# A two-layer hybrid block: the feed-forward's down product by Strassen's scheme over squares kept in DRAM, and the states of the linear attention formed before its outputs

## The chip, the cores and the metric

The kernel runs on one core of a Trainium2 chip. The metric is the time of one execution on the device in microseconds (us), as the median of several runs.

## The reference

The input is 1024 tokens of width 1024, in float32. Two layers of a first block and one layer of a second block follow each other. A layer of the first block mixes tokens (gated linear attention and latent softmax attention) and then has a feed-forward part with squared ReLU. The change lies in the feed-forward and in the linear attention of this block.

```python
def first_block(x, c, positions, ...):
    cos, sin = rope_tables(positions)
    for l in range(DEPTH):                                   # DEPTH = 2
        shift_a, scale_a, gate_a, shift_f, scale_f, gate_f = ...
        h = rms_norm(x) * (1.0 + scale_a) + shift_a
        x = x + gate_a * hybrid_mixer(h, cos, sin, ...)
        h = rms_norm(x) * (1.0 + scale_f) + shift_f
        x = x + gate_f * (jnp.square(jax.nn.relu(h @ w_mlp_up[l])) @ w_mlp_down[l])

# linear attention, chunk by chunk (heads of 64 keys and 128 values):
#   o = (q exp(b)) state + attn v;   state = exp(b_last) state + k_dec^T v
```

`w_mlp_up` is 1024 x 4096 and `w_mlp_down` 4096 x 1024 in each layer. The second block (dilated attention and long convolutions) is not touched.

## The kernel before

Activations lie transposed: 8 tiles of 128 features, each in two halves of 512 tokens (`hf`). Every large product is made from three matmuls: an operand is split into a high part (`split_hi`, ACT) and the rest (`split_lo`, a subtraction, POOL unless told otherwise), and high x high, high x low and low x high are summed in PSUM. One matmul covers 128 x 128 weights and 512 tokens.

The program is traced in the order of the source and a planner then orders each engine's instructions by readiness in its own model of time, with ties to the earlier one. On the chip each engine runs its list in that fixed order and waits on semaphores. DMAs are issued from SP's queue and from ACT's queue.

The feed-forward is `mlp`, called at the end of `layer1`. It goes through the 4096 hidden features in 16 chunks of 256. For a chunk, `up_weights` loads and splits two 1024 x 128 blocks of weights, `up_part` makes four products of 24 matmuls, takes ReLU (ACT), multiplies by the PSUM value (DVE) and splits the square at once (ACT, POOL). `down_weights` loads and splits two 128 x 1024 blocks, and `down_part` makes 16 products of 6 matmuls, each of which DVE scales by a gate and adds to the residual `x[f, hf]`. The down part of a chunk runs behind the up part of the next, so that up and down alternate; the last chunk is written out by hand, with `state[0](0)`, the norm of token half 0 for the next layer (`enter`), in between.

Linear attention is `gla`: 8 steps over (256 tokens, head pair). A step runs `gla_chunks` for this step with `gla_decays` of the next step beside it, and one piece of the mixer's output projection (`project_out`) is drawn in at every yield. In `gla_chunks` two chunks of 128 tokens follow each other (`cc`): score matmuls into `A`, evictions into `scores`, output products into `o_ps`, outer products into `u_ps`, from which DVE forms the new state. The two `u_ps` products of a chunk share one PSUM bank, and each is read by DVE before the next is written.

The rope tables (`rope_tables`) stay in SBUF through both layers.

Of the kernel before, what the change touches and what calls it, by code (L numbers as in the profile page):

```python
# [147 lines left out]
class Kernel:  # L148
# [285 lines left out]
    def block1(self):  # L434
        nc, i = self.nc, self.i
        self.mods = {}
        cond = self.cond_cols(i["c"], True, "1")
        cond2 = self.cond_cols(i["c_2"], False, "2")
        self.ada = {"0": (cond, i["w_ada"][0], i["b_ada"][0]), "1": (cond, i["w_ada"][1], i["b_ada"][1]),
                    "2": (cond2, i["w_ada_2"][0], i["b_ada_2"][0])}  # L440
        self.eps5 = self.C.tile([128, 1], F32, name="eps5")
        nc.gpsimd.memset(self.eps5, 1e-5)
        rp, rclose = self.open("rope", "right")
        xp, xclose = self.open("x0", "right")
        with self.pool("mod_0", "right") as p:
            x = self.load_x(xp)
            self.rope_tables(rp)
            self.main_tables()

            self.rstds = {hf: self.norm_rstd(p, x, hf, keep=2) for hf in range(2)}  # L450
            self.drain(self.modulation(p, "0", (0, 1), 10, True))
            state = self.enter("a0", x, self.mods["0", 1], self.mods["0", 0])
            self.first_weights(0)
            for hf in range(2):
                state[0](hf)
        for l in range(2):
            nxt = (lambda x, w: self.enter("a1", x, self.mods["1", 1], self.mods["1", 0], wclose=w)) if l == 0 else \
# [3 lines left out]
            state, xclose = self.layer1(l, state, xclose, nxt)  # L461
        xclose()
        rclose()
        return state

    def layer1(self, l, state, xclose, enter_next):
        nc, i = self.nc, self.i
        _, H, xs, close = state
        xclose()
        mixd = self.DR.tile([2, 8, 2, 128, 512], F32, name=f"mix{l}")  # L470

        ap, aclose = self.open("mla_in", "right")
        A = self.project_latent(l, H, ap)
# [14 lines left out]
        with self.pool("mod") as p:  # L488
            mods = (("0", (2, 3, 4, 5)), ("1", (0, 1))) if l == 0 else (("1", (2, 3, 4, 5)), ("2", (0, 1, 2)))
            fill = (None for name, secs in mods for _ in self.modulation(p, name, secs))  # L490
            steps = 8 * sum(len(secs) for _, secs in mods)
# [11 lines left out]
            for n in range(34):  # L503
                h, i = divmod(n, 8)
# [8 lines left out]
                if n > 1:  # L513
                    h, i = divmod(n - 2, 8)
# [6 lines left out]
        tclose()  # L521
        paclose()
        aclose()

        xp, xclose = self.open("x", "right")
        xa = {(f, hf): xp.tile([128, 512], F32, name=f"xa{f}_{hf}") for hf in range(2) for f in range(NF)}
# [25 lines left out]

        mp, mpclose = self.open("mlp", "right")
        hp, hclose = self.open("h2_0")
        hq, hqclose = self.open("h2_1", "right")
        H = {}
        self.h_tiles(H, hp, "f", 0)
        self.h_tiles(H, hq, "f", 1)
# [8 lines left out]
        def close():  # L567
            hclose()
            return enter_next(xa, wclose)

        return self.mlp(l, H, xa, gate_f, mp, close, lambda: (hqclose(), mpclose())), xclose

    def project_out(self, l, mp, mixd, part, xa, gate, tag, bufs, halves=(0, 1)):

# [22 lines left out]
        for _ in steps:  # L597
            pass

    def mlp(self, l, H, x, gate, p, close, pclose):  # L600

        nc, i = self.nc, self.i
        up, down = i["w_mlp_up"][l], i["w_mlp_down"][l]
        pt, ptclose = self.open("mlp_even", "right")

        def up_part(c, w, mt, hf):
            ps = self.PS.tile([128, 512], F32, name="up", tag="mm", bufs=2)
            self.gemm(ps, w[mt], slice(0, 128), lambda k, h: H[k, h], 8, hf)
            sq = p.tile([128, 512], F32, name="relu2", tag="relu2", bufs=2)
            nc.scalar.activation(sq, ps, AF.Relu)  # L610
            nc.vector.tensor_mul(sq, ps, sq)  # L611
            hi, lo = ((p if c % 2 else pt).tile([128, 512], F32R, name="act", tag=f"act{b}", bufs=4) for b in range(2))
            self.split_hi(hi, sq)
            self.split_lo(lo, sq, hi)
            return hi, lo

        def down_weights(c):
            dw = []
            for mt in range(2):
                n0 = c * 256 + mt * 128  # L620
                raw = pt.tile([128, 1024], F32, name="dn_raw", tag="dnr", bufs=2)
                nc.sync.dma_start(raw, down[n0 : n0 + 128, :])
                hi = p.tile([128, 1024], F32R, name="dn_hi", tag="dnh", bufs=3)
                lo = p.tile([128, 1024], F32R, name="dn_lo", tag="dnl", bufs=3)
                self.split_hi(hi, raw)
                self.split_lo(lo, raw, hi)
                dw.append((hi, lo))
            return dw

        def down_part(dw, act, hf):  # L630
            for f in range(NF):
                ps = self.PS.tile([128, 512], F32, name="dn", tag="dn", bufs=4)
                n = 0
                for mt in range(2):
                    (wh, wl), (ah, al) = dw[mt], act[mt, hf]
                    for a, b in ((wh, ah), (wh, al), (wl, ah)):
                        self.mm(ps, a[:, f * 128 : (f + 1) * 128], b, n == 0, n == 5)
                        n += 1
                nc.vector.scalar_tensor_tensor(x[f, hf], ps, gate[:, f : f + 1], x[f, hf], op0=ALU.mult, op1=ALU.add)  # L639
# [5 lines left out]
        behind = None  # L645
        for c in range(15):
            w, act = up_weights(c), {}

            for mt, hf in ((0, 0), (1, 0), (0, 1), (1, 1)) if c == 0 else ((0, 0), (0, 1), (1, 0), (1, 1)):
                act[mt, hf] = up_part(c, w, mt, hf)  # L650
            if behind:
                for hf in range(2):
                    down_part(*behind, hf)
            behind = down_weights(c), act
        w, act = up_weights(15), {}
        for mt in range(2):
            act[mt, 0] = up_part(15, w, mt, 0)
        for hf in range(2):
            down_part(*behind, hf)
        dw = down_weights(15)  # L660
        ptclose()
        state = close()
        down_part(dw, act, 0)
        state[0](0)
        for mt in range(2):
            act[mt, 1] = up_part(15, w, mt, 1)
        down_part(dw, act, 1)
        pclose()
        self.psum(f"ps_in{l}")
        state[0](1)  # L670
        return state
# [159 lines left out]
    def gla_setup(self, l, p, A):  # L831
# [15 lines left out]
        for b in range(2):  # L847
            nc.gpsimd.memset(heads[64 * b : 64 * b + 64, b : b + 1], 1.0)

        G["state"] = [[p.tile([128, 2, 128], F32, name=f"state{hp}_{n}") for n in range(2)] for hp in range(2)]  # L850
# [80 lines left out]
    def gla_chunks(self, p, G, oT, g, hp):  # L931
# [19 lines left out]
        group = []  # L951
        for cc in range(2):
            c = 2 * g + cc
            ct = slice(cc * 128, cc * 128 + 128)
            S_prev, sn = G["state"][hp][c % 2], G["state"][hp][1 - c % 2]

            z = G.pop(("z", g, hp, cc))
            ps = self.PS.tile([128, 1024], F32, name="A", tag="big", bufs=2)
# [15 lines left out]
            if cc:  # L974
                yield
            for b in range(2):
                h = 2 * hp + b
                if c:
                    group.append(self.mm(o_ps[:, b, cc, :], S_prev[:, b], e[:, cc, 7, :], True, False))
                group.append(self.mm(o_ps[:, b, cc, :], v[:, cc, h * 128 : h * 128 + 128], a[:, b], c == 0, True))  # L980
            if c < 7:
                u_ps = self.PS.tile([128, 128], F32, name="u_ps", tag="sm", bufs=2, padded_shape=[128, 512])
                for b in range(2):
                    r = slice(64 * b, 64 * b + 64)
                    h = 2 * hp + b
                    self.mm(u_ps[r], kd[:, cc * 128 + b * 64 : cc * 128 + b * 64 + 64], v[:, cc, h * 128 : h * 128 + 128],
                            True, True, tile_position=(0, 64 * b))
                    if c == 0:
                        nc.vector.tensor_copy(sn[r, b], u_ps[r])
                    else:  # L990
                        nc.vector.scalar_tensor_tensor(sn[r, b], S_prev[r, b], el[r, cc : cc + 1], u_ps[r], op0=ALU.mult, op1=ALU.add)
        self.in_order(group)
        for b in range(2):
            h = 2 * hp + b
# [1108 lines left out]
```

## Time and profile before

| | |
|---|---|
| median of 3 runs | 4408.63 us (4402.69 to 4411.74) |
| profiled execution, its own time | 4400.58 us |
| its span, first to last instruction | 4398.7 us |
| mean granted clock of the tensor engine | 0.966 |
| instructions | 52184 |

The profile is one execution. Its page has busy times by engine; the views behind it group instructions by line and shape, list them in order of time, sum up what waited for what, and give busy time by window. PE is the tensor engine's matmuls, PEld its weight loads (beside the matmuls), DVE VectorE, ACT ScalarE, POOL GpSimd, SP the engine whose queue issues most DMAs. Matmuls overlap in the pipeline, so the duration of one is longer than the distance from one start to the next.

### The profile page before, as it was taken

The numbers are of one execution on the slowest core, as the hardware profiler recorded it, in microseconds if no ns is written. First come the engines' busy times: TensorE is split into PE (matmuls) and PEld (weight loads), VectorE is DVE, ScalarE is ACT, GpSimd is POOL, SyncE is SP. The second block draws the span as 40 slices with busy tenths as digits, with TensorE's granted clock in tenths as the row PEclk, the third lists the DMA queues.
The fourth block names the chain that finished last, engine by engine and source line by source line (L and its number), as shares of the span: only waits on it lengthen the run. The fifth ranks groups of instructions, "written<-read, shape, count | busy, mean of one in ns | idle before, by whom it ended". The sixth has DMA issues, their size and how long they took to land. (4 is left out here: it accounts for less than half of the span.)

```text
span 4398.7 us, 52184 instructions
## 1 busy us (share of the span) xinstructions
PE 4077.9 (93%) x19748; PEld 3195.0 (73%) x19748; DVE 2020.7 (46%) x3789; ACT 1447.4 (33%) x2722; POOL 1419.1 (32%) x1309
## 2 busy tenths in 40 slices
PE   6999888999999999888999999899999999899788
PEld 3776666888887685566788888567777777778666
DVE  5427675333334515577433333652221444567446
ACT  5435354121212525444312121322223445211222
POOL 3322455333333422155433333212221111244242
PEclk8999899999999999999999999999999999999899
DMA  6245543111111126643211111144445332444353
GB/s 188 68 135 159 161 131 106 47 49 48 48 48 42 55 84 196 178 136 116 78 47 49 48 48 44 61 123 116 117 103 138 101 94 78 139 144 143 130 180 110
DMA packets 566222, 449.84 MB, mean 102 GB/s; under 512 B 197384, under 2 KB 468702, under 8 KB 565970
## 3 DMA queue, kind: packets, MB, share of 16 engines
q1 hardware_dynamic: 375514, 352.68, 26.3%
q10 hardware_dynamic: 189880, 92.63, 7.3%
q8 instruction: 156, 2.56, 0.2%
q0 software_dynamic: 576, 1.18, 0.1%
q14 instruction: 96, 0.79, 0.1%
HBM read 342.87 MB, written 100.92 MB: 101 GB/s over the span
## 5 line engine op out<-in xcount | busy, mean ns | idle before, releaser
L200 POOL TENSOR_TENSOR w_lo<-w_raw,w_hi 128x1024 fp32r<-128x1024 f32 (+4 forms) x237 | 449.1, 1896 | 1132.7 <-ACT w_hi L194 1111.1
L191 PE MATMUL dn<-act,dn_hi 128*128 128x512 f32 x2048 | 637.5, 392 | 14.5 <-DVE xa L639 6.0
L639 DVE SCALAR_TENSOR_TENSOR xa<-dn,mod,xa 128x512 f32<-128x512 f32 x512 | 383.7, 750 | 273.0 <-PE dn L191 271.2
L191 PE MATMUL in<-b2h,w_hi 128*128 128x512 f32 x1152 | 474.5, 412 | 5.6 <-ACT qkv_t L1650 5.6
L194 ACT ACTIVATE w_hi<-w_raw 128x1024 fp32r<-128x1024 f32 (+4 forms) x276 | 237.1, 860 | 710.6 <-PE in L191 271.5
L191 PE MATMUL in<-b2l,w_hi 128*128 128x512 f32 x1152 | 459.7, 399 | 0.0
L191 PEld LDWEIGHTS dn<-act,dn_hi 128*128 128x128 f32 x2048 | 386.8, 189 | 100.1 <-DVE xa L639 7.6
L191 PE MATMUL in<-b2h,w_lo 128*128 128x512 f32 x1152 | 458.4, 398 | 0.0
L191 PE MATMUL up<-fh,w_hi 128*128 128x512 f32 x1024 | 406.8, 397 | 0.4 <-DVE relu L611 0.4
L191 PE MATMUL up<-fl,w_hi 128*128 128x512 f32 x1024 | 404.0, 395 | 1.6 <-POOL fl L200 1.3
L191 PE MATMUL dn<-act,dn_lo 128*128 128x512 f32 x1024 | 402.0, 393 | 2.8 <-POOL dn_lo L200 2.8
L191 PE MATMUL up<-fh,w_lo 128*128 128x512 f32 x1024 | 404.2, 395 | 0.0
L611 DVE TENSOR_TENSOR relu<-up,relu 128x512 f32<-128x512 f32 x128 | 88.5, 691 | 610.1 <-ACT relu L610 610.1
L200 POOL TENSOR_TENSOR dn_lo<-dn_raw,dn_hi 128x1024 fp32r<-128x1024 f32 x64 | 152.1, 2398 | 525.1 <-ACT dn_hi L194 525.0
L191 PEld LDWEIGHTS in<-b2h,w_hi 128*128 128x128 f32 x1152 | 221.5, 192 | 64.6 <-issue 12.2
L191 PEld LDWEIGHTS in<-b2h,w_lo 128*128 128x128 f32 x1152 | 220.8, 192 | 53.4 <-issue 6.4
L191 PEld LDWEIGHTS in<-b2l,w_hi 128*128 128x128 f32 x1152 | 221.4, 192 | 47.4 <-issue 4.4
L194 ACT ACTIVATE dn_hi<-dn_raw 128x1024 fp32r<-128x1024 f32 x64 | 64.8, 1053 | 554.3 <-PE dn L191 546.8
L191 PEld LDWEIGHTS up<-fl,w_hi 128*128 128x128 f32 x1024 | 192.8, 188 | 49.2 <-POOL fl L200 3.0
L191 PEld LDWEIGHTS up<-fh,w_hi 128*128 128x128 f32 x1024 | 192.9, 188 | 46.3 <-issue 1.7
L191 PEld LDWEIGHTS dn<-act,dn_lo 128*128 128x128 f32 x1024 | 193.9, 189 | 44.5 <-POOL dn_lo L200 3.6
L191 PEld LDWEIGHTS up<-fh,w_lo 128*128 128x128 f32 x1024 | 192.9, 188 | 45.5 <-issue 1.0
(488 smaller groups left out, 7871.1 us busy)
## 6 DMA issues: line engine op xcount, KB each, us to landing
wada<-in_w_ada SPq DMA_DIRECT2D x120, 512.0 KB
w_raw<-in_w_in SPq DMA_DIRECT2D x102, 512.0 KB
w_raw<-in_w_mlp_up SPq DMA_DIRECT2D x64, 512.0 KB
dn_raw<-in_w_mlp_down SPq DMA_DIRECT2D x64, 512.0 KB
qkv<-qkv_t ACTq DMA_DIRECT2D x72, 256.0 KB
w_raw<-in_w_out SPq DMA_DIRECT2D x64, 256.0 KB
mix<-mix SPq DMA_DIRECT2D x64, 256.0 KB
spectra<-spec ACTq DMA_DIRECT2D x32, 384.0 KB
```

The costliest lines, as they stand in the source:

```text
L191: return self.nc.tensor.matmul(out, lhsT, rhs, start=start, stop=stop, **kw)
L194: self.nc.scalar.activation(hi, x, AF.Copy, **kw)
L200: return eng.tensor_sub(lo, x, hi.bitcast(F32))
L611: nc.vector.tensor_mul(sq, ps, sq)
L639: nc.vector.scalar_tensor_tensor(x[f, hf], ps, gate[:, f : f + 1], x[f, hf], op0=ALU.mult, op1=ALU.add)
```

## The change

The feed-forward falls into two parts. First all 16 chunks of the up product run, and their squares are written to a DRAM tensor `actd` from ACT's queue, unsplit. Then the down product runs over blocks of 512 hidden features: `raws` loads four weight blocks `A[m, k]` (output half, contraction half) and four blocks of squares `B[k, t]` (contraction half, token half). For seven blocks `products` forms Strassen's seven pairs (Winograd's form, with eight sums and differences on DVE) and `exact` splits every operand, in a ring of three buffers, two pairs ahead of the matmuls. Each pair gives 4 tiles of 6 matmuls, which DVE adds to 28 accumulators `acc` (ACT copies them for the first block). The eighth block is multiplied plainly, and the accumulators are combined in between (`self.plus`, which shares sums between DVE and POOL by a running count of cost, and `gated`).

In the linear attention the outer products and state updates of both chunks of a step move ahead of the second chunk's scores, and all output products come after the yield. A third state buffer holds the state in between.

For room in SBUF the rope tables go to DRAM at the start, are closed before the linear attention of layer 0, and are loaded again for layer 1.

```diff
+            self.rope_spill = self.DR.tile([2, 128, S], F32, name="rope_spill")
+            for n, t in enumerate((self.rc, self.rs)):
+                nc.scalar.dma_start(self.rope_spill[n], t)
...
+        if l:
+            rp, rclose = self.open("rope", "right")
...
+            for n, t in enumerate((self.rc, self.rs)):
+                nc.sync.dma_start(t, self.rope_spill[n])
...
+        actd = self.DR.tile([32, 2, 128, 512], F32, name=f"act{l}")
...
+        def up_part(kt, w, hf):
+            ps = self.PS.tile([128, 512], F32, name="up", tag="dn", bufs=4)
             self.gemm(ps, w, slice(0, 128), lambda k, h: H[k, h], 8, hf)
+            sq = sp.tile([128, 512], F32, name="relu2", tag="relu2", bufs=4)
             nc.scalar.activation(sq, ps, AF.Relu)
             nc.vector.tensor_mul(sq, ps, sq)
-            self.split_hi(hi, sq)
-            self.split_lo(lo, sq, hi)
+            nc.scalar.dma_start(actd[kt, hf], sq)
...
+        def raws(c):
+            A, B = {}, {}
+            yield A, B
+            for m, k, t in ((0, 0, 0), (0, 1, 0), (1, 1, 1), (1, 0, 1)):
+                kt = 4 * c + 2 * k
+                pool, tag, bufs = (dp, "dnr", 3) if m == 0 else (self.W, "wr", 2) if k else (dp, "dnr1", 2)
+                A[m, k] = pool.tile([128, 2, 512], F32, name="dn_raw", tag=tag, bufs=bufs)
+                nc.sync.dma_start(A[m, k], down[kt * 128 : kt * 128 + 256, m * 512 : m * 512 + 512].rearrange("(j p) n -> p j n", p=128))
+                B[k, t] = dp.tile([128, 2, 512], F32, name="sq_raw", tag="sqr", bufs=6)
+                nc.sync.dma_start(B[k, t], actd[kt : kt + 2, t].rearrange("j p n -> p j n"))
+                yield
...
+        def products(A, B):
+            V = nc.vector
+            yield 0, exact("a", A[0, 0], lo_vector=True), exact("b", B[0, 0], lo_vector=True)
+            yield 1, exact("a", A[0, 1]), exact("b", B[1, 0])
+            a22, b22 = exact("a", A[1, 1]), exact("b22", B[1, 1], True)
+            V.tensor_sub(B[0, 0], B[0, 1], B[0, 0])
+            V.tensor_sub(B[0, 1], B[1, 1], B[0, 1])
+            V.tensor_sub(B[1, 1], B[1, 1], B[0, 0])
+            V.tensor_sub(B[1, 0], B[1, 0], B[1, 1])
+            yield 3, a22, exact("b", B[1, 0])
+            V.tensor_add(A[1, 1], A[1, 0], A[1, 1])
+            V.tensor_sub(A[1, 0], A[0, 0], A[1, 0])
+            V.tensor_sub(A[0, 0], A[1, 1], A[0, 0])
+            V.tensor_sub(A[0, 1], A[0, 1], A[0, 0])
+            yield 2, exact("a", A[0, 1]), b22
+            yield 4, exact("a", A[1, 1]), exact("b", B[0, 0])
+            yield 5, exact("a", A[0, 0]), exact("b", B[1, 1])
+            yield 6, exact("a", A[1, 0]), exact("b", B[0, 1])
...
+        def work(c, p, w, a):
+            for f in range(4):
+                ps = multiply(f, [(w, a)])
+                if c:
+                    nc.vector.tensor_add(acc[p, f], ps, acc[p, f])
+                else:
+                    nc.scalar.activation(acc[p, f], ps, AF.Copy)
...
+        for f in range(4):
+            self.plus(acc[1, f], acc[0, f], acc[1, f])
+            gated(f, 0, acc[1, f])
+            self.plus(acc[5, f], acc[0, f], acc[5, f])
+            self.plus(acc[6, f], acc[5, f], acc[6, f])
+            self.plus(acc[3, f], acc[6, f], acc[3, f])
+            gated(4 + f, 0, acc[3, f])
+        for f in range(4):
+            plain(f, 0)
+        wa[1, 0], wa[1, 1], sb[0, 1] = exact("a", A[1, 0]), exact("a22", A[1, 1], True), exact("b", B[0, 1])
+        for f in range(4, 8):
+            plain(f, 0)
+        for f in range(4):
+            self.plus(acc[5, f], acc[4, f], acc[5, f])
+            self.plus(acc[2, f], acc[5, f], acc[2, f])
+            gated(f, 1, acc[2, f])
+            self.plus(acc[6, f], acc[4, f], acc[6, f])
+            gated(4 + f, 1, acc[6, f])
...
+        state = enter_next()
         state[0](0)
+        sb[1, 1] = exact("b", B[1, 1])
+        for f in range(8):
+            plain(f, 1)
```

In `gla_chunks`:

```diff
-            S_prev, sn = G["state"][hp][c % 2], G["state"][hp][1 - c % 2]
...
+            scores.append(a)
+            if cc == 0:
+                for c in (2 * g, 2 * g + 1):
+                    S_prev, sn = states[c % 3], states[(c + 1) % 3]
+                    if c == 7:
+                        break
+                    u_ps = self.PS.tile([128, 128], F32, name="u_ps", tag="sm", bufs=2, padded_shape=[128, 512])
+                    for b in range(2):
...
+        yield
+        for cc in range(2):
+            c = 2 * g + cc
             for b in range(2):
                 h = 2 * hp + b
                 if c:
+                    group.append(self.mm(o_ps[:, b, cc, :], states[c % 3][:, b], e[:, cc, 7, :], True, False))
+                group.append(self.mm(o_ps[:, b, cc, :], v[:, cc, h * 128 : h * 128 + 128], scores[cc][:, b], c == 0, True))
```

## Rows read from the trace of the kernel before

**Rows 1.** The page: busy us, share of the span, instructions, by engine.
```profile
PE 4077.9 (93%) x19748; PEld 3195.0 (73%) x19748; DVE 2020.7 (46%) x3789; ACT 1447.4 (33%) x2722; POOL 1419.1 (32%) x1309
```

**Rows 2.** By window, layer 1: stretch, us; PE, PEld, DVE, ACT, POOL; clock, DMA.
```profile
2200.00:2400.00 200.00, 200.00 (x876) 164.05 (x875) 67.72 (x92) 38.57 (x52) 64.66 (x35) 1.00 0.16 48
```

**Rows 3.** Timeline of ACT (start, us, what): a weight split in two following chunks.
```profile
1310.84 1.06 ACT L194 ACTIVATE dn_hi<-dn_raw 128x1024 fp32r<-128x1024 f32 x1 [18.18 <-PE dn L191]
...
1354.79 1.06 ACT L194 ACTIVATE dn_hi<-dn_raw 128x1024 fp32r<-128x1024 f32 x1 [18.18 <-PE dn L191]
```

**Rows 4.** Groups by line and shape: count, busy us, mean ns, idle before.
```profile
L639 DVE SCALAR_TENSOR_TENSOR xa<-dn,mod,xa 128x512 f32<-128x512 f32 x512 | 383.7, 750 | 273.0 <-PE dn L191 271.2
L611 DVE TENSOR_TENSOR relu<-up,relu 128x512 f32<-128x512 f32 x128 | 88.5, 691 | 610.1 <-ACT relu L610 610.1
L200 DVE TENSOR_TENSOR w_lo<-w_raw,w_hi 128x1024 fp32r<-128x1024 f32 x28 | 34.3, 1225 | 227.2 <-ACT w_hi L194 227.2
L1540 DVE TENSOR_TENSOR nacc<-nacc,nsq 128x512 f32<-128x512 f32 x27 | 22.8, 845 | 1.2
L200 POOL TENSOR_TENSOR act<-relu,act 128x512 fp32r<-128x512 f32 x128 | 168.1, 1314 | 171.0 <-ACT act L194 171.0
L200 POOL TENSOR_TENSOR dn_lo<-dn_raw,dn_hi 128x1024 fp32r<-128x1024 f32 x64 | 152.1, 2398 | 525.1 <-ACT dn_hi L194 525.0
L194 ACT ACTIVATE dn_hi<-dn_raw 128x1024 fp32r<-128x1024 f32 x64 | 64.8, 1053 | 554.3 <-PE dn L191 546.8 <-DMA dn_raw<-in_w_mlp_down 7.5
```

**Rows 5.** Timelines of POOL and DVE where both run, layer 0 of the feed-forward.
```profile
1413.80 1.70 POOL L200 TENSOR_TENSOR a1l<-nt,a1h 128x512 fp32r<-128x512 f32 x1 [3.23 <-ACT a1h L194]
1415.47 1.71 POOL L200 TENSOR_TENSOR act<-relu,act 128x512 fp32r<-128x512 f32 x1
1417.14 2.82 POOL L200 TENSOR_TENSOR w_lo<-w_raw,w_hi 128x1024 fp32r<-128x1024 f32 x1
...
1412.37 0.74 DVE L307 SCALAR_TENSOR_TENSOR a1l<-nt,mod,a1h 128x512 fp32r<-128x512 f32 x1
...
1414.29 6.22 DVE L299 SCALAR_TENSOR_TENSOR nt<-xa,s_a,rstd 128x512 f32<-128x512 f32 x3
...
1334.86 2.41 POOL L200 TENSOR_TENSOR w_lo<-w_raw,w_hi 128x1024 fp32r<-128x1024 f32 x1 [3.14 <-ACT w_hi L194]
...
1335.85 1.55 DVE L639 SCALAR_TENSOR_TENSOR xa<-dn,mod,xa 128x512 f32<-128x512 f32 x2
```

**Rows 6.** PE after two waits near the end of layer 0, and windows behind.
```profile
1391.10 0.50 PE L191 MATMUL dn<-act,dn_lo 128*128 128x512 f32 x1 [1.38 <-POOL dn_lo L200]
...
1417.23 0.80 PE L191 MATMUL dn<-act,dn_hi 128*128 128x512 f32 x1 [2.30 <-POOL act L200]
...
1392.00:1400.00 8.00, 8.00 (x37) 6.62 (x36) 6.94 (x11) 3.78 (x6) 0.00 (x0) 1.00 0.46 170
1418.00:1421.00 3.00, 3.00 (x9) 2.33 (x8) 3.00 (x2) 1.46 (x3) 3.00 (x2) 0.50 0.00 0
1430.00:1436.00 6.00, 6.00 (x28) 4.98 (x27) 4.30 (x7) 1.27 (x2) 0.00 (x0) 1.00 0.69 255
```

**Rows 7.** Waits of PE, 1385 to 1440 us: in total, times, longest.
```profile
PE dn L191 <- ACT act L194: 4.1, 2, 3.7
PE dn L191 <- POOL act L200: 2.7, 2, 2.3
```

**Rows 8.** Linear attention: PE waits of the span, two timeline pieces, a window.
```profile
PE u_ps L191 <- DVE state L991: 16.3, 8, 3.4
...
518.96 0.69 PE L191 MATMUL u_ps<-gv,kdec 128*64 128x128 f32 x2 [3.40 <-DVE state L991]
...
527.92 0.43 PE L191 MATMUL u_ps<-gv,kdec 128*64 128x128 f32 x2
...
520.00:525.00 5.00, 5.00 (x14) 3.94 (x13) 2.33 (x11) 1.41 (x2) 1.66 (x6) 0.50 0.00 0
```

**Rows 9.** By window, start of the kernel: the last two columns are DMA.
```profile
20.00:40.00 20.00, 13.21 (x107) 6.62 (x107) 17.74 (x24) 15.46 (x22) 7.92 (x4) 0.84 1.04 396
```

More of the change, by code (lines that the diff above doesn't have):

```diff
@@ L630, in down_part @@
[L630 to L639, printed above, removed]
+            nc.scalar.dma_start(actd[kt, hf], sq)
@@ L655, in mlp @@
[L655 to L663, printed above, removed]
-        state[0](0)
[L665 to L668, printed above, removed]
+        def raws(c):
[9 more added lines that the diff above has]
+                yield
@@ new lines, in mlp, with exact @@
+        turns = {}
+        def exact(name, raw, own=False, lo_vector=False):
+            if not own:
+                n = turns[name] = (turns.get(name, -1) + 1) % 3
+            if own:
+                pool, tag, bufs = dx, "22", 1
+            elif n == 2:
+                pool, tag, bufs = dx, name, 1
+            elif name == "a":
+                pool, tag, bufs = self.W, "", 2
+            else:
+                pool, tag, bufs = dp, name, 2
+            hi = pool.tile([128, 2, 512], F32R, name=f"{name}_hi", tag="wh" + tag, bufs=bufs)
+            lo = pool.tile([128, 2, 512], F32R, name=f"{name}_lo", tag="wl" + tag, bufs=bufs)
+            self.split_hi(hi, raw)
+            self.split_lo(lo, raw, hi, "v" if lo_vector else False)
+            return hi, lo
@@ new lines, in multiply, with gated @@
+        def multiply(f, pairs):
+            ps = self.PS.tile([128, 512], F32, name="dn", tag="dn", bufs=4)
+            n, last = 0, 6 * len(pairs) - 1
+            for (wh, wl), (ah, al) in pairs:
+                for j in range(2):
+                    for a, b in ((wh, ah), (wh, al), (wl, ah)):
+                        self.mm(ps, a[:, j, f * 128 : f * 128 + 128], b[:, j], n == 0, n == last)
+                        n += 1
+            return ps
+        def gated(f, hf, y):
+            nc.vector.scalar_tensor_tensor(x[f, hf], y, gate[:, f : f + 1], x[f, hf], op0=ALU.mult, op1=ALU.add)
@@ new lines, in mlp @@
+        blocks = load = None
+        for c in range(16):
+            w = up_weights(c)
+            if c == 15:
+                load = raws(0)
+                blocks = next(load)
+                self.drain(load)
+            for mt, hf in ((0, 0), (1, 0), (0, 1), (1, 1)) if c == 0 else ((0, 0), (0, 1), (1, 0), (1, 1)):
+                up_part(2 * c + mt, w[mt], hf)
+        spclose()
+        hclose()
+        dx, dxclose = self.open("mlp_third", "right")
+        ap, apclose = self.open("mlp_acc", "right")
@@ new lines, in mlp, with steps @@
+        acc = {(p, f): ap.tile([128, 512], F32, name=f"acc{p}_{f}") for p in range(7) for f in range(4)}
+        def steps():
+            nonlocal blocks, load
+            for c in range(7):
+                A, B = blocks
+                for n, (p, w, a) in enumerate(products(A, B)):
+                    if n == 3:
+                        load = raws(c + 1)
+                        blocks = next(load)
+                    if n in (3, 5):
+                        next(load)
+                    if n > 4:
+                        next(load, None)
+                    yield c, p, w, a
@@ new lines, in work @@
+        def work(c, p, w, a):
[3 more added lines that the diff above has]
+                    nc.vector.tensor_add(acc[p, f], ps, acc[p, f])
+                else:
+                    nc.scalar.activation(acc[p, f], ps, AF.Copy)
+        ahead = []
+        for step in steps():
+            ahead.append(step)
+            if len(ahead) > 2:
+                work(*ahead.pop(0))
+        for step in ahead:
+            work(*step)
+        A, B = blocks
@@ new lines, in mlp, with plain @@
+        wa, sb = {}, {}
+        for k in range(2):
+            wa[0, k], sb[k, 0] = exact("a", A[0, k]), exact("b", B[k, 0])
+        def plain(f, hf):
+            gated(f, hf, multiply(f % 4, [(wa[f // 4, k], sb[k, hf]) for k in range(2)]))
+        for f in range(4):
[5 more added lines that the diff above has]
+            gated(4 + f, 0, acc[3, f])
@@ L848, in gla_setup @@
             nc.gpsimd.memset(heads[64 * b : 64 * b + 64, b : b + 1], 1.0)
-        G["state"] = [[p.tile([128, 2, 128], F32, name=f"state{hp}_{n}") for n in range(2)] for hp in range(2)]
+        G["state"] = [[p.tile([128, 2, 128], F32, name=f"state{hp}_{n}") for n in range(3)] for hp in range(2)]
         for t in G["state"][0] + G["state"][1]:
@@ L950, in gla_chunks @@
         o_ps = self.PS.tile([128, 2, 2, 128], F32, name="o_ps", tag="o", bufs=1)
-        group = []
+        group, scores, states = [], [], G["state"][hp]
         for cc in range(2):
```

74 lines of the change are left out of this document (23 added, 51 removed).

## The prediction

> **What bounds the kernel now.** I read the page's busy times first. The tensor engine (PE) is busy for 93% of the span, VectorE (DVE) for 46%, ScalarE (ACT) for 33%, GpSimd (POOL) for 32% [rows 1]. Then came the stretch that the change rewrites, the feed-forward of a layer. There PE is busy 200.00 of 200 us at the full granted clock, while DVE does 68 and POOL 65 [rows 2]. So the stretch lasts as long as its matmuls, and the price of one is what counts. The listed durations (0.39 us) overlap and are no price. The chunk period is: the same weight split starts at 1310.84 and at 1354.79, and 43.95 us for a chunk's 96 up and 96 down products make 0.2289 us each [rows 3]. After that I took the durations on the other engines, because the change moves work onto them [rows 4], what DVE and POOL do to each other [rows 5], what a wait does to PE's clock [rows 6], the waits at the end of a feed-forward [rows 7], the waits in linear attention [rows 8] and what the DMA engines can carry [rows 9].
>
> **Part 1: fewer matmuls.** The down product of a layer is 1536 matmuls before. After, seven of eight blocks of the contraction take seven products of 24 instead of eight, 7 x 7 x 24 = 1176, and the last block stays plain with 192. That is 1368, so 168 fewer in a layer and 336 in all: 336 x 0.2289 = **-76.9 us**, all of it on the path, since PE never rests there [rows 2, 3]. The up part keeps its 1536 matmuls and its splits. Its squares now go out on ACT's queue and come back on SP's: 1 MB in 22 us of up part and 4 MB in 38.5 us of down part, some 110 GB/s, where a stretch of this trace moved 396 GB/s [rows 9]. Three to six buffers cover the loads, so I cost them at nothing; with the cover gone a 512 KB load would show at 1.3 us (0.512 MB over that rate).
>
> **Part 2: what the other engines do per block of seven products.** PE needs 168 x 0.2289 = 38.45 us. ACT has 14 splits of 1.05 us, 15 us. POOL has 12 differences of 2.40 us, 28.8 us. DVE has 28 additions from PSUM (0.69 us, by the square that also reads PSUM and SBUF), eight sums and differences of raw blocks and two splits of 1024 columns (1.225 us): 19.3 + 12.3 = 31.6 us [rows 4]. Every sum is below 38.45, but no longer far below, and two engines are not independent. Where both run instructions with two SBUF inputs they take turns: from 1414.29 three DVE instructions that otherwise take 0.74 us took 6.22 us, one per POOL instruction, and POOL's 1.31 and 2.40 grew to 1.70 and 2.82 [rows 4, 5]. So a DVE instruction beside a 1024-column POOL one waits up to 2.82 - 0.74 = 2.1 us. The additions from PSUM have one SBUF input; two gated ones of that kind that ran beside a POOL split took 1.55 us together, no more than their mean of 0.75 each [rows 4, 5].
>
> The Trainium skill (SBUF — State Buffer, section "Who interferes with whom") speaks against the change here: the port pair that DVE and GpSimd share is an exclusive lock, and a DVE instruction with two SBUF inputs and a GpSimd instruction that reads SBUF shut each other out for the whole instruction. The trace agrees that they take turns, but not for the whole: 1.67 us from one POOL start to the next with a DVE instruction in between, where whole turns would be 1.31 + 0.74 = 2.05 [rows 4, 5].
>
> Where the wait bites: the raw sums stand together, four before the third product and four before the fourth, and the additions that free PSUM's four banks queue behind them on DVE. From the second-last product of a block to the second of the next, three products long (72 x 0.2289 = 16.5 us), DVE must get through the eight sums (9.8 us) and nine additions (6.2 us), 16.0 us, before PE finds its next bank. Alone it just fits: 0. Five POOL splits lie in that time. If each stops a raw sum for the full 2.1 us, the block waits 16.0 + 10.3 - 16.5 = 9.8 us; that is the other end. I take half, since a sum arrives somewhere within a POOL instruction and two of the five have no rival on DVE ready: 16.0 + 5.1 - 16.5 = 4.6 us. The first block of a layer is copied by ACT and has slack, so 6 blocks x 2 layers x 4.6 = **+55 us** (0 to 118).
>
> The clock: after 1.38 us of waiting PE kept the upper of its two levels (granted 1.00, 2.4 GHz), after 2.30 us it ran at the lower level (granted 0.50, 1.2 GHz), and it was back at 1.00 by 1430 [rows 6]. A stretch at 0.50 held 14 matmuls in 5.00 us instead of 3.2, 1.8 us lost [rows 8]. A wait of 4.6 us is probably two of some 2.3; I let a third of the twelve fall: 4 x 1.8 = **+7 us** (0 to 22).
>
> **Part 3: the ends of the feed-forward.** Gone are the waits on the last up part's squares, in layer 0 4.1 + 2.7 us and 1.4 us on a weight split, plus the low clock after them [rows 6, 7]. New are the 44 closing sums a layer; before the first plain products 16 `plus` (some 11 of them on DVE at 0.85, a neighbouring two-input row) and 8 gated ones (0.75) make 15.3 us against 4 banks x 12 x 0.2289 = 11.0 us of cover, so 4.3 us late; and the last split (1.05 + 2.40 us) stands between two halves of plain products behind only 1.4 us of matmuls, 2.1 us late [rows 4]. Old and new cancel: **0** (-8 to +20 for both layers). The rope tables go out at the start, 1 MB at 396 GB/s, 2.6 us of a saturated stretch [rows 9], and come back before layer 1 on SP, where the loads of its first weights are queued behind them; those weights have the last plain products as cover, and without it the two loads cost another 2.6 us. I take **+2 us** (0 to 5).
>
> **Part 4: linear attention.** PE waits eight times, 16.3 us, for the state update that frees the bank of the next outer product, the longest 3.40 us and followed by the lower clock [rows 8]. In the change both outer products stand among the score matmuls of the second chunk, ahead of the next step's decays on DVE, as the first chunk's already does, where PE does not wait [rows 8]. If half of the eight also cost 1.8 us of clock, that is 16.3 + 4 x 1.8 = **-23 us**. The ends are 0 (the waits come back at the output products, which now all stand behind the yield) and -31 (all eight with clock).
>
> **Sum:** -76.9 + 55 + 7 + 0 + 2 - 23 = -36 us on the profiled execution's 4400.6 us, 4364.6. The median of the runs is 8 us above that execution, so I say **4372 us**; its own range, with block waits of 2 to 7 us, is 4340 to 4402.
>
> **Rivals.** (a) *DVE becomes the bound, slower.* Every raw sum meets a POOL split and the additions stand behind it: 9.8 us a block and the clock falls each time: -76.9 + 118 + 22 + 2 - 23 = +42, 4451 us. It decides from 7.6 us a block on, where the 91 us of the other terms are used up. For it: POOL would be busy 75% and DVE 82% of a block. Against it: part of POOL's work waits for those very sums. (b) *The turns cost nothing*, because the planner's order keeps sums and splits apart: -76.9 + 2 - 23 = -98, 4311 us. For it: POOL rests while it waits for PE to free a buffer. (c) *The two engines exclude each other wholly*, so that a block lasts 12 x 2.40 + 10 x 1.225 = 41.05 us, 2.6 more than PE needs: 14 x 2.6 = 36, in sum -62, 4347 us. This is the lock rule of the Trainium skill's SBUF page named above. Against it: the 1.67 us. (d) *The state change does not do what it says*: DVE gets the updates late all the same, 0 for -23: 4395 us.
>
> **How the numbers follow.** Chances: forecast 0.36, (a) 0.22, (b) 0.18, (c) 0.14, (d) 0.10. What a measurement of this kernel can tell from no change is about 0.2%, that is 4399.8 to 4417.4 us. Faster by more: nearly all of the forecast, (b), (c) and half of (d), less a little of (a)'s lower end on the other side: 0.65. Within: 0.13. Slower: 0.22. The range goes from (b) to (a), 4310 to 4450, which leaves out the tails of both.
>
> **What would show it.** Matmuls on the page fall by 336. Right: in the down part PE's granted clock stays mostly at 1.00 and the largest waits read PE `dn` <- DVE `acc`, 2 to 7 us a block. For (a): DVE busy near 100% there, its raw sums at 2 us and more instead of 1.225. For (b): PE without gaps at 38.5 us a block. For (c): 41 us a block with POOL never idle. The row `u_ps` <- `state` should be gone; if `o_ps` shows as much, it is (d). Wrong altogether if loads of squares, or POOL's splits in a chain, end the waits.

## The result: 0.73% slower

The changed kernel takes 4437.91 us (median of 6 runs, 4433.19 to 4449.25), the kernel before in the same comparison 4409.28 us. The ratio is 1.0073, 95% interval 1.0059 to 1.0087. The forecast was 4372 us and faster. The time lies outside the forecast's own range (4340 to 4402), inside the wider one that takes in its rivals (4310 to 4450), and on the other side of no change.

The page of after, first line of busy times (as in [rows 1]), and then the largest waits of PE that concern the change (what was waited for: us in all, times, longest):

```profile
PE 4036.5 (91%) x19412; PEld 3135.6 (71%) x19412; DVE 2223.9 (50%) x3855; ACT 1544.1 (35%) x2798; POOL 1624.1 (37%) x1323
```

```profile
PE dn L191 <- DVE acc L726: 51.8, 55, 1.8
PE wo L191 <- DVE xa L598: 25.3, 15, 3.1
...
PE ms L191 <- DVE nacc L1649: 16.0, 6, 5.6
PE dn L191 <- ACT b_hi L194: 15.5, 3, 7.2
...
PE dn L191 <- DVE xa L690: 9.9, 3, 4.3
PE dn L191 <- POOL b_lo L200: 8.8, 5, 2.9
...
PE u_ps L191 <- DVE state L1092: 2.6, 2, 2.1
```

The 336 matmuls are gone (19748 to 19412), and PE waits instead: for the additions that free PSUM's banks, for splits, and for the norm's sums `nacc`.

Windows of after, layer 0 (columns as in [rows 2]): the end of the up part and the seam to the down part, a block of seven products, the seventh block, the entry to the next layer.

```profile
1060.00:1080.00 20.00, 20.00 (x89) 16.31 (x88) 4.85 (x5) 8.94 (x15) 6.50 (x3) 1.00 0.11 41
1080.00:1110.00 30.00, 21.36 (x78) 16.25 (x77) 9.67 (x6) 15.22 (x21) 23.45 (x10) 0.77 0.42 131
1190.00:1230.00 40.00, 36.44 (x154) 28.05 (x153) 34.55 (x36) 13.73 (x14) 28.71 (x12) 1.00 0.29 91
1338.00:1390.00 52.00, 42.73 (x174) 31.35 (x173) 48.23 (x44) 15.03 (x16) 43.25 (x17) 1.00 0.18 47
...
1455.00:1470.00 15.00, 9.38 (x28) 4.96 (x26) 8.06 (x7) 8.90 (x15) 9.41 (x5) 0.77 0.30 84
```

In the block DVE is busy 34.55 and POOL 28.71 of 40 us, and PE 36.44 with the clock still at 1.00: many short waits. At the seam PE works 21.36 of 30 us, and the granted clock has a mean of 0.77 there, so it stood at its lower level (1.2 GHz) for part of it. In the seventh block DVE is busy 93% and POOL 83% of the time.

Where DVE's time goes, DVE's timeline of one block and POOL's beside it. L664 to L667 are the sums of squares, L669 to L672 those of weights, L726 the additions from PSUM:

```profile
1157.72 1.21 DVE L664 TENSOR_TENSOR sq_raw<-sq_raw 128x1024 f32<-128x1024 f32 x1
...
1201.42 1.21 DVE L664 TENSOR_TENSOR sq_raw<-sq_raw 128x1024 f32<-128x1024 f32 x1
1202.55 1.27 DVE L726 TENSOR_TENSOR acc<-dn,acc 128x512 f32<-128x512 f32 x2
1203.75 2.23 DVE L665 TENSOR_TENSOR sq_raw<-sq_raw 128x1024 f32<-128x1024 f32 x1
1205.91 0.68 DVE L726 TENSOR_TENSOR acc<-dn,acc 128x512 f32<-128x512 f32 x1
1206.51 2.82 DVE L666 TENSOR_TENSOR sq_raw<-sq_raw 128x1024 f32<-128x1024 f32 x1
```

```profile
1202.47 2.43 POOL L200 TENSOR_TENSOR a_lo<-dn_raw,a_hi 128x1024 fp32r<-128x1024 f32 x1 [4.99 <-ACT a_hi L194]
1204.85 3.40 POOL L200 TENSOR_TENSOR b_lo<-sq_raw,b_hi 128x1024 fp32r<-128x1024 f32 x1
1208.21 3.38 POOL L200 TENSOR_TENSOR a_lo<-dn_raw,a_hi 128x1024 fp32r<-128x1024 f32 x1
```

A sum that meets no split takes 1.21 us, one that does 2.2 to 2.8 in these middle blocks, and the split beside it 3.40 where it took 2.40 before [rows 4]. L664 recurs after 43.70 us: one block of 168 matmuls takes what 192 took before (43.95, [rows 3]).

The time of each block, from the start of its first `dn` matmul to that of the 168th behind it on PE's timeline, in us. The last column is the first 168 of the plain block's 192 matmuls, with the norm between:

| kernel, layer 0 | first | 2 | 3 | 4 | 5 | 6 | seventh | plain |
|---|---|---|---|---|---|---|---|---|
| after | 51.3 | 42.0 | 43.5 | 43.8 | 43.7 | 43.6 | 51.1 | 56.6 |
| e3: no raw sums | 40.8 | 38.9 | 38.7 | 38.9 | 38.9 | 38.7 | 44.2 | 57.3 |
| e4: no splits on POOL | 43.4 | 38.9 | 38.7 | 38.9 | 38.9 | 38.7 | 38.9 | 47.7 |
| e5: sums in the up part | 38.9 | 38.9 | 38.7 | 38.9 | 38.9 | 38.7 | 44.2 | 58.7 |
| e7: splits in halves | 49.9 | 42.2 | 42.0 | 42.5 | 42.3 | 42.0 | 42.9 | 62.1 |
| e9: paced, new order | 38.9 | 38.9 | 38.7 | 38.9 | 38.9 | 38.7 | 50.7 | 44.3 |

And the stages between first matmuls of a kind, layer 0 / layer 1, in us:

| | before | after | e4 | e5 | e8 | e9 |
|---|---|---|---|---|---|---|
| linear attention, first `D` to first `up` | 229.2 / 230.4 | 226.5 / 227.5 | 228.9 / 222.9 | 226.5 / 223.1 | 227.2 / 225.7 | 227.7 / 228.8 |
| feed-forward, first `up` to the next stage's first product | 726.5 / 740.0 | 736.1 / 748.9 | 684.4 / 694.6 | 715.2 / 728.6 | 687.5 / 700.9 | 688.3 / 696.9 |
| of it the up part alone | - | 354.9 / 354.7 | 354.7 / 354.7 | 373.8 / 373.8 | 355.2 / 355.4 | 354.7 / 354.7 |
| entry: first `ga_ps` to `g_ps` / first `in` to `f_ps` | 61.6 / 28.6 | 71.3 / 36.0 | 69.7 / 35.9 | 71.4 / 36.0 | 70.0 / 36.2 | 69.9 / 33.1 |

Of the 32.7 us between the profiled executions of before and after the feed-forward carries 18.5, the two entries 17.1 and the linear attention -5.6; the rest, 2.7 us, is shifts of either sign, among them 7.8 us later at the start of layer 0's linear attention.

### The profile page after: what moved, and what is told of

Read it like the earlier page. It is cut to its first block, busy times and chain, and to the rows that moved or that the text cites. A ratio compares the mean times of both kernels' runs of the same rounds, so it can differ in the third digit from the quotient of the medians.

```text
span 4431.4 us, 52371 instructions
## 1 busy us (share of the span) xinstructions
PE 4036.5 (91%) x19412; PEld 3135.6 (71%) x19412; DVE 2223.9 (50%) x3855; ACT 1544.1 (35%) x2798; POOL 1624.1 (37%) x1323
## 5 line engine op out<-in xcount | busy, mean ns | idle before, releaser
L191 PE MATMUL dn<-b_hi,a_hi 128*128 128x512 f32 x912 | 372.6, 410 | 77.3 <-DVE acc L726 51.8
L191 PE MATMUL dn<-b_lo,a_hi 128*128 128x512 f32 x912 | 366.0, 401 | 8.8 <-POOL b_lo L200 8.8
L191 PE MATMUL dn<-b_hi,a_lo 128*128 128x512 f32 x912 | 363.7, 399 | 0.0
L200 POOL TENSOR_TENSOR a_lo<-dn_raw,a_hi 128x1024 fp32r<-128x1024 f32 x92 | 238.1, 2596 | 158.7 <-ACT a_hi L194 158.7
L191 PEld LDWEIGHTS dn<-b_hi,a_hi 128*128 128x128 f32 x912 | 174.3, 191 | 148.8 <-DVE acc L726 47.2
L200 POOL TENSOR_TENSOR b_lo<-sq_raw,b_hi 128x1024 fp32r<-128x1024 f32 x92 | 260.3, 2837 | 36.7 <-ACT b_hi L194 36.7
L726 DVE TENSOR_TENSOR acc<-dn,acc 128x512 f32<-128x512 f32 x336 | 221.2, 681 | 73.0 <-PE dn L191 73.0
L194 ACT ACTIVATE a_hi<-dn_raw 128x1024 fp32r<-128x1024 f32 x106 | 110.8, 1059 | 335.2 <-DVE dn_raw L672 103.4
L191 PE MATMUL wo<-mix,w_hi 128*128 128x512 f32 x512 | 186.5, 439 | 44.5 <-DVE xa L598 25.3
L191 PEld LDWEIGHTS up<-fl,w_hi 128*128 128x128 f32 x1024 | 192.8, 188 | 42.5 <-POOL fl L200 1.8
```

Source lines behind the costliest of these rows:

```text
L191: return self.nc.tensor.matmul(out, lhsT, rhs, start=start, stop=stop, **kw)
L194: self.nc.scalar.activation(hi, x, AF.Copy, **kw)
L200: return eng.tensor_sub(lo, x, hi.bitcast(F32))
L726: nc.vector.tensor_add(acc[p, f], ps, acc[p, f])
```

## Experiments

### The two halves of the change

e1 puts the new `gla_chunks` and the third state buffer into the kernel before; e2 does the reverse in the changed kernel; e11 does it in the best kernel below (e9).

```diff
-G["state"] = [[p.tile([128, 2, 128], F32, name=f"state{hp}_{n}") for n in range(2)] ...
+G["state"] = [[p.tile([128, 2, 128], F32, name=f"state{hp}_{n}") for n in range(3)] ...
 (and gla_chunks as in the change; e2 and e11 the other way round)
```

> The kernel before with the new order of the linear attention alone. Forecast on record: -23 us, 4386. Theory after the result: the waits u_ps <- state go (16.3 to about 2.6 us) but wo <- xa and others grow, and only some 6 us stay: 4403 (3 us a layer from the first decays to the first up matmul). Rival that the state change does nothing: 4409.

> The changed kernel with the old order of the linear attention, so the feed-forward and the rope tables alone. Theory: the feed-forward costs the whole difference and a little more, 4438 + 6 = 4444. Forecast of the linear attention at -23: 4461. If both parts add, e1 and e2 give the change's +29 us together.

> The paced kernel with the new product order, with the linear attention of the kernel before. The new order of the attention was worth 6 us in the kernel before and 14 us in the changed kernel. Theory, that it is worth about 10 us wherever it stands: 4343. If it is 6: 4339; if the forecast's 23 us hold here: 4356.

Measured: e1 4402.09 us beside 4407.91, ratio 0.9987 (0.9975 to 1.0000); e2 4452.15, 1.0101 (1.0085 to 1.0118); e11 4348.23, against 4333.47 for e9. So by the medians the new order is worth 6, 14 and 15 us: the theory's 6 held in e1, its 4444 for e2 was too low, and e11 lies between its 4343 and the forecast's 4356. The medians of a pair come from different comparisons. Each kernel beside its own kernel before, the new order is worth some 6, 12 and 16 us, each known only to some 6 to 11 us by the intervals, so the three may be one value. The parts do not quite add: -6 and +44 make +38 where the change has +29, a difference of about the size of the noise. Two of PE's waits in e1, and the first of them in before (the second is in [rows 8], 16.3 us):

```profile
PE wo L191 <- DVE xa L593: 26.2, 15, 4.0
...
PE u_ps L191 <- DVE state L989: 4.2, 2, 2.1
```

```profile
PE wo L191 <- DVE xa L593: 18.5, 10, 3.8
```

The wait for the state falls by 12.1 us, and the output projection drawn in beside it waits 7.7 us longer for DVE. So more than half of what the waits gave is given back there.

### Who takes turns with whom: e3 and e4

```diff
 e3, products():                       e4, exact():
-V.tensor_sub(B[0, 0], ...)            -self.split_lo(lo, raw, hi, "v" if lo_vector else False)
-... (all eight)                       +if lo_vector: self.split_lo(lo, raw, hi, "v")
                                       +else: self.split_hi(lo, raw)
```

> The changed kernel with the eight sums and differences of raw blocks left out (products take raw blocks as they are, so the output is another). Theory of turns: the block of seven products falls from 43.7 us to 38.5 to 39, 12 blocks x 4.7 = -57, and the first block of a layer gains some 3 us: 4375 to 4380. Rival, that POOL's chain of splits or the additions from PSUM bound the block: it stays above 42 us, 4418 or more.

> The changed kernel with the low parts of the down product's operands written by ACT as a plain copy in place of POOL's subtraction (two low parts a block stay on DVE); the low parts are wrong by it, and POOL has nothing to do in the blocks. DVE's work is unchanged. Theory of turns: raw sums take 1.22 us each, the block is 38.5 to 39.5 us, 4380. Rival, that DVE's own 31.6 us of work in bursts of four sums is what PE waits for: the block stays above 42 us, 4425 or more.

Measured: e3 4358.23 us, ratio 0.9886 (0.9868 to 0.9904); e4 4326.48, 0.9818 (0.9799 to 0.9838). Both lay below what the theory gave, since it counted the blocks and too little of the seam and the ends. A block in e4 and in e3 by window:

```profile
1190.00:1230.00 40.00, 40.00 (x175) 32.39 (x173) 30.43 (x41) 26.66 (x29) 0.00 (x0) 1.00 0.35 105
```

```profile
1195.00:1235.00 40.00, 40.00 (x175) 32.39 (x174) 22.14 (x31) 14.62 (x15) 29.75 (x13) 1.00 0.34 105
```

PE is full in both, in e4 with all of DVE's sums and in e3 with all of POOL's splits. Neither alone is in the way; it takes both. The groups of e4, of after and of e3:

```profile
L729 DVE TENSOR_TENSOR acc<-dn,acc 128x512 f32<-128x512 f32 x336 | 228.0, 689 | 109.6 <-PE dn L191 108.0
...
L669 DVE TENSOR_TENSOR sq_raw<-sq_raw 128x1024 f32<-128x1024 f32 x14 | 17.1, 1218 | 0.0
```

```profile
L200 POOL TENSOR_TENSOR b_lo<-sq_raw,b_hi 128x1024 fp32r<-128x1024 f32 x92 | 260.3, 2837 | 36.7 <-ACT b_hi L194 36.7
...
L726 DVE TENSOR_TENSOR acc<-dn,acc 128x512 f32<-128x512 f32 x336 | 221.2, 681 | 73.0 <-PE dn L191 73.0
...
L666 DVE TENSOR_TENSOR sq_raw<-sq_raw 128x1024 f32<-128x1024 f32 x14 | 37.4, 2671 | 0.2
```

```profile
L200 POOL TENSOR_TENSOR b_lo<-sq_raw,b_hi 128x1024 fp32r<-128x1024 f32 x92 | 225.2, 2448 | 0.0
```

Without POOL's splits the third sum of squares (L669 of e4, L666 of after) takes 1.22 us, with them 2.67; without the sums POOL's split takes 2.45, with them 2.84. The additions from PSUM cost 0.68 to 0.69 us in both. And e4's row of the table shows that the turns price more than the blocks: with no split on POOL the first block falls by 7.9 us, the seventh by 12.2, the plain block by 8.9. Of the 51.7 us by which the feed-forward of layer 0 is shorter (736.1 to 684.4), some 22.5 lie in blocks 2 to 6. In the first and the plain block e4 does not tell the turns from the length of POOL's splits, which it takes out as well (a low part takes ACT 1.05 us and POOL 2.40).

### Length of one turn: e7 and e10

```diff
-self.split_lo(lo, raw, hi, "v" if lo_vector else False)
+if lo_vector: self.split_lo(lo, raw, hi, "v")
+else:
+    for j in range(2):
+        self.split_lo(lo[:, j], raw[:, j], hi[:, j])
```

e7 is this in the changed kernel, e10 in e9 below.

> The changed kernel with each of POOL's splits in the down part as two instructions of 512 columns. POOL's work grows from 28.8 to some 31.5 us a block. Theory, that what counts is how long a DVE sum waits for the POOL instruction it meets: raw sums 2.2 to 2.8 become 1.7 to 2.0 us, block 43.7 to 41 or 42 us, 4410 to 4420. Rival, that the time both engines need the port in sum counts: block as before or longer, 43.7 to 45, 4438 to 4455.

> The paced kernel with the new product order, and POOL's splits of the down part as two instructions of 512 columns. In the blocks there is nothing left to gain (38.8 us). Theory, that the wait of a DVE sum is the rest of the POOL instruction it meets: seventh block 48 to 51 us becomes 45 to 48, 4325 to 4330. Rival, that POOL's larger sum of work costs as much at the ends: 4333 to 4340.

Measured: e7 4414.92 us, ratio 1.0023 (1.0012 to 1.0034); e10 4333.02, 0.9843 (0.9822 to 0.9865), as e9. Two groups of e7:

```profile
L200 POOL TENSOR_TENSOR b_lo<-sq_raw,b_hi 128x512 fp32r<-128x512 f32 x184 | 300.2, 1655 | 7.7 <-ACT b_hi L194 6.8
...
L670 DVE TENSOR_TENSOR sq_raw<-sq_raw 128x1024 f32<-128x1024 f32 x14 | 24.2, 1726 | 2.5 <-POOL b_lo L200 2.3
```

POOL's work grows (92 splits of 2.84 us, 260 us, become 300), and still the third sum falls from 2.67 to 1.73 us and the block from 43.6 to 42.2. In the blocks the wait of a single sum counts, and it goes with the length of the instruction that it meets. The larger part of e7's gain lies in the seventh block (51.1 to 42.9), and the plain block gives 5.5 us of it back (56.6 to 62.1). In e10, where no sums are left in the blocks, the same edit brings nothing: in layer 0 the seventh block falls from 50.7 to 48.9 us, and the plain block rises from 44.3 to 47.7.

### The sums where both engines rest: e5, e6, e8

e5 forms all eight sums in the up part, stores them and loads them; e6 also splits six of the plain block's eight operands there; e8 puts each load of a down weight for this behind the up weights of its chunk in SP's queue, two loads a chunk, and forms the sums of weights a chunk later.

```diff
 e5, after the up products of a pair of chunks:
+V.tensor_sub(b00, b01, b00)  ... (four of squares, four of weights)
+for n, s in enumerate((b00, b01, b11, b10)):
+    nc.scalar.dma_start(bsum[c, n], s)
 e6:
+split_early(n, raw)          # split_hi, split_lo, both stored; loaded as they are for the plain block
 e8:
+self.in_order([self.last_load, dma])
```

> The changed kernel, with the eight sums and differences of raw blocks formed in the up part, where DVE and POOL rest, and kept in DRAM; the down part loads them. Nothing is left out. Theory of turns: the down part runs as without the sums (block 38.8 us, first block 41, seventh 44), the up part stays at its matmuls (355 us a layer), 4358, and 4365 if the up part pays some 3 us a layer. Rival, that the seven loads a side and block (186 GB/s) or the stores (125 GB/s beside the weights) show: a block at 41 us or more, or an up part of 365 us, 4400.

> The kernel with the sums in the up part, and six of the eight operands of the plain block split in the up part too and loaded as high and low part, so that POOL has two splits left where DVE forms the closing sums. Theory of turns: seventh block 44 to 40 us, the plain block's first 168 matmuls 57 to 50 us, some 8 us a layer: 4342. Rival, that the ends wait for DVE's own work of closing sums and norm: within 3 us of the kernel with the sums in the up part alone.

> The kernel with the sums in the up part and most of the plain block split early, with each load of a down weight put behind the up weights of the same chunk on SP's queue. In the run without this order the planner issued them all in the first 180 us of the up part, where the DMA engines moved 340 to 390 GB/s and up weights came late: up part 375 us a layer in place of 355. Theory: the up part is back at 355 to 358 us, -18 x 2 us: 4347. Rival, that the extra stores on ACT's queue or DVE's sums delay the squares: up part stays above 368, 4370 or more.

Measured: e5 4401.48 us, ratio 0.9994 (0.9985 to 1.0002); e6 4383.84, 0.9952 (0.9939 to 0.9965); e8 4344.57, 0.9858 (0.9842 to 0.9875). In e5 the blocks came out as expected (the first even at 38.9 where 41 were expected), but the up part took 373.8 us in place of 354.9. ACT's timeline there shows how (ACTq are the DMAs that ACT issues), and DVE's the sum that it waits for. Below are a window of e5, the same window of e8, and one of e6:

```profile
814.01 11.94 ACTq L643 DMA_DIRECT2D asum<-dn_raw  x2
826.00 0.60 ACT L622 ACTIVATE sq_raw<-up 128x512 f32<-128x512 f32 x1 [11.75 <-DVE dn_raw L638]
```

```profile
824.37 1.23 DVE L638 TENSOR_TENSOR dn_raw<-dn_raw 128x1024 f32<-128x1024 f32 x1 [9.39 <-DMA dn_raw<-in_w_mlp_down]
```

```profile
816.00:836.00 20.00, 15.04 (x60) 11.58 (x59) 7.32 (x7) 2.14 (x3) 3.41 (x2) 0.88 1.00 361
```

```profile
816.00:836.00 20.00, 20.00 (x90) 16.57 (x89) 10.83 (x10) 4.64 (x6) 6.09 (x3) 1.00 0.92 337
```

```profile
876.00:896.00 20.00, 18.50 (x69) 15.04 (x70) 10.40 (x11) 4.77 (x7) 4.77 (x2) 0.83 0.93 339
```

The loads of down weights, which wait for free buffers alone, had all been issued early, by 856 us, 140 us into the up part; a store on ACT's queue waited for its sum and that for its load, and a ReLU and a split of up weights stood behind it. In e8 the DMA engines move nearly as much (337 beside 361 GB/s), and PE is full; e6, which differs from e8 in this pacing alone, moves 339 in its window, and PE misses 1.5 us and runs at a granted clock of 0.83 in the mean. What cost time was what stood behind whom, not the rate alone. e6 has a plain block of 49.3 us in place of 58.7, so POOL's last splits were a part of the ends; its up part, 376.2 us, was no shorter than e5's, and its seventh block stayed at 44.2 us where the theory had 40, so the kernel missed the 4342. e8 has the up part back at 355.2 us and lies at 4345, where the theory had 4347.

### The closing sums: e9

```diff
-yield 1, ...; yield 3, ...; yield 2, ...; yield 4, ...; yield 5, ...; yield 6, ...
+for p in (5, 1, 6, 3, 4, 2):
+    yield p, exact("a"), exact("b")
...
 the closing sums, regrouped to fit the order:
-self.plus(acc[6, f], acc[5, f], acc[6, f])
-self.plus(acc[3, f], acc[6, f], acc[3, f])
+self.plus(acc[3, f], acc[6, f], acc[3, f])
+self.plus(acc[3, f], acc[5, f], acc[3, f])
```

> As the paced kernel, with the products of a block in the order 0, 5, 1, 6, 3, 4, 2, so that some 24 of the 44 closing sums can run during the seventh block. Theory, that the ends of the down part wait for the burst of closing sums: seventh block about 44 us as before, the plain block 4 to 8 us a layer shorter, 10 us below the paced kernel. Rival, that the closing sums only move the wait into the seventh block, beside POOL's splits: the same time as the paced kernel within 5 us.

Measured: 4333.47 us, ratio 0.9830 (0.9813 to 0.9846), 11 us below e8 in the median, but with intervals that touch and profiled spans of 4335.0 and 4332.3 us. The traces speak mostly for the rival: the plain block falls from 49.6 to 44.3 us in layer 0, and the seventh rises from 44.2 to 50.7; in layer 1 they go from 56.2 to 49.7 and from 44.3 to 47.5. The wait moves into the seventh block, and 3 us of it go in layer 1. Which of e8 and e9 is faster stays open; both beat the kernel before, by 1.4% and 1.7%.

## Why the prediction was wrong, point by point

In the profiled executions -35.9 us were forecast and +32.7 came, 68.6 more. By term: the blocks of seven products +37 (the first and the seventh blocks and a slightly dearer matmul, less a clock term that did not come), the linear attention +17, the entry to the next stage +17, the ends inside the feed-forward -4, the rest +1.

**Fewer matmuls, -76.9 us: right.** 336 are gone. Where PE never waits (e3, e4, e5) a block takes 38.73 to 38.92 us where 38.45 were worked out, 5 us over 14 blocks.

**Turns in a block, +4.6 us each: right in mechanism and size, wrong in reach.** In blocks 2 to 6 the loss against 38.8 is 22.5 us in layer 0, 4.5 a block. From block 3 on five of a block's eight sums take 2.2 to 2.8 us and three 1.21, 16.5 us in all, 6.8 more than alone. The forecast took 5.1, and gave two of five splits no rival; so its 4.6 agrees more closely than the terms behind it, which is in part luck. The additions from PSUM did not grow, and `dn` <- `acc` leads the waits at 51.8 us. The clock's +7 us did not come in these blocks: the granted clock is 1.00 in their windows, and it fell at the seam.

**"The first block of a layer is copied by ACT and has slack": this step failed.** The first block lost 12.5 us in each layer. The copies do have slack, but POOL's first four splits stand before the last sums of squares, and these before the split of the third product. In after, DVE's sum, ACT's split that waits for it, PE's two waits there, and PE's window behind:

```profile
1081.69 3.36 DVE L666 TENSOR_TENSOR sq_raw<-sq_raw 128x1024 f32<-128x1024 f32 x1
...
1086.10 1.21 DVE L667 TENSOR_TENSOR sq_raw<-sq_raw 128x1024 f32<-128x1024 f32 x1
```

```profile
1087.35 2.00 ACT L194 ACTIVATE b_hi<-sq_raw 128x1024 fp32r<-128x1024 f32 x2 [5.46 <-DVE sq_raw L667]
```

```profile
PE dn L191 <- ACT b_hi L194: 7.2, 1, 7.2
PE dn L191 <- POOL b_lo L200: 1.4, 1, 1.4
```

```profile
1085.00:1090.00 5.00, 1.54 (x4) 1.16 (x4) 4.67 (x5) 2.20 (x3) 1.52 (x1) 0.50 0.35 105
```

The waits are 8.6 us, and PE starts again at the lower level of its clock. Three sums grow to 3.4 us in this block, by 2.2, a little over the 2.1 that the forecast took for the most. Without the raw sums the block takes 40.8 us, with the sums made earlier 38.9. Splits in a chain that end the waits were the forecast's own sign of being wrong.

**Seventh block.** The forecast gave it 4.6 us like the others; it lost 12.2. Without the raw sums it takes 44.2 us (e3, e5), so 6.9 of the 12.2 go with them. The other 5.4 go with POOL's splits (e4: 38.9 us): the closing sums, which have two SBUF inputs as well, meet them there. First, middle and seventh blocks together lost 94 us in both layers, where the forecast had 55 + 7; the forecast's own point of turning, 7.6 us on 12 blocks, is 91. So rival (a) came true in its sum, by another division than its "every sum meets a split".

**The ends: 0, in fact +13 for both layers, inside the range -8 to +20.** Inside the feed-forward old and new did cancel: beyond blocks and matmuls, before loses 23.3 us in layer 0 (726.5 - 3072 x 0.2289), after 21.5 (736.1 - 2904 x 0.2289 - 49.9 lost in the blocks). What came on top is the entry to the next stage, 9.7 and 7.4 us. The forecast did not look beyond the last product: this step failed too. There half 1 is normed: ACT squares, DVE adds the squares up in `nacc`, and PE reads it for `ms`. In layer 0, before and then after:

```profile
1433.91 0.64 ACT L1534 ACTIVATE nsq<-xa 128x512 f32<-128x512 f32 x1 [7.97 <-DMA x_spill_a<-xa]
...
1437.18 2.27 DVE L1540 TENSOR_TENSOR nacc<-nacc,nsq 128x512 f32<-128x512 f32 x3
...
1439.51 1.12 PE L191 MATMUL ms<-nacc,ones_d 128*128 128x512 f32 x2 [0.51 <-DVE nacc L1540]
```

```profile
1454.40 1.65 ACT L1643 ACTIVATE nsq<-xa 128x512 f32<-128x512 f32 x3
...
1457.13 2.59 POOL L200 TENSOR_TENSOR w_lo<-w_raw,w_hi 128x1024 fp32r<-128x1024 f32 x1 [0.17 <-POOL w_lo L200]
...
1457.62 4.24 DVE L1649 TENSOR_TENSOR nacc<-nacc,nsq 128x512 f32<-128x512 f32 x3
...
1461.91 2.08 PE L191 MATMUL ms<-nacc,ones_d 128*128 128x512 f32 x2 [5.62 <-DVE nacc L1649]
```

The last down product starts its last matmul at 1436.1 us in before and at 1450.9 in after, so `ms` comes 3.4 and 11.1 us behind it. In before the squares begin 2 us ahead of that point, in after 3.5 us behind it; and in after POOL splits weights of the next stage beside the additions, three of which take 4.24 us for 2.27. So turns show here too, of another pair than in the down part, and the entry stays longer without splits in the down part (e4: 69.7 and 35.9 us).

**Linear attention, -23 us: over-sized.** The waits went as foretold (16.3 to 2.6), and the rival's `o_ps` did not grow in their place (4.1 us on `scores` in before, 3.1 in after). But 16.3 us of waits were taken as 16.3 us of time, with clock on top. `wo` <- `xa` grew from 18.5 to 25.3, and by their medians the runs give 6, 14 and 15 us; the stage itself is 5.6 us shorter in after. The step that failed is that nothing was named that is late next.

**Rope tables, +2 us.** No run separates them; the 2.7 us outside the named stages leave room for them.

**Rivals (b) and (c).** e4 takes the splits away and so stands for (b), 4326 against the 4311 worked out. That they lie close is in part luck: in the traces the entries are 15 us longer, the linear attention gains 8 us instead of 23 and the blocks lose 14, while the ends inside the feed-forward are 25 us shorter than in before. For (c) the lock rule of the Trainium skill (SBUF — State Buffer, "Who interferes with whom") would have a split and a sum exclude each other wholly: 2.40 + 1.21 = 3.61 us from split to split. The trace has 3.36 (from 1204.85 to 1208.21, rows above): nearly whole turns, 0.25 us of overlap where the forecast's pair of rows had 0.38.

**Open.** Why the linear attention's start in layer 0 comes 1 to 11 us later in all kernels with the two parts (483.5 to 491.5 us, against 480.6 and 482.1) was not tried; the first products of the layer start at the same time (47.6 to 51.6 us, before 49.9), and each figure is from one execution, while runs of one kernel differ by up to some 30 us. In after the 8 us arise late: the last product of `qpe_ps` starts at 343.4 us where it started at 343.5, and `D` starts at 488.4 where it started at 480.6. Why half 1 is normed later at the entry was not tried. And whether the new attention order is worth more in the changed kernels than the 6 us in the kernel before is not settled; the stage itself, both layers together, is shorter by 6.7, 13.4 and 10.9 us in the three pairs of traces.

## To carry to other kernels

Where two engines take turns, price every stretch in which their two-input instructions meet, the first and the last round of a loop and the entry to the next stage most of all: here they cost more than the ten middle blocks. Work whose inputs are ready early can go where those engines rest, and here that paid even for a trip through DRAM; but its loads and stores need an order that keeps them from standing in front of the loop's own. Of a wait that goes, name what is late next before it is counted as time.

## What the runs showed of the hardware

Two things were not expected. Halving POOL's instructions made them dearer in sum (260 to 300 us for the splits of the squares) and the kernel still 0.5% faster, since DVE's sums got their turn sooner. And a stretch in which the DMA engines moved 337 GB/s (e8) cost PE nothing, where one with 339 (e6) cost it 1.5 of 20 us and one with 361 (e5) 5: the order in the queues made the difference.
